# PSUM banks of a mixture-of-experts scatter: from a pool of three to a pool of five

## The chip, the core and the metric

The kernel runs on one core of one Trainium2 chip. Its time is the device time of one launch in microseconds (us). Three runs of the kernel before gave 1573.3, 1576.45 and 1577.18 us; their median is 1576.45 us. TensorE is written PE, VectorE DVE, ScalarE ACT, GpSimd POOL, SyncE SP.

## The reference, cut to what matters

Two layers, each with a mixer, a mixture of experts (MoE) and a gated embedding, over 512 tokens of width 1024. The MoE, which takes most of the time, is this:

```python
expert = g_top * EXPERTS_PER_GROUP + top_i          # 2 of 32 experts for each token
weight = pg_top * top_p
...
def expert_block(args):
    idx, e = args
    xb = x_pad[idx]                                  # gather
    hb = jax.nn.silu(xb @ w_gate[e]) * (xb @ w_up[e])
    return hb @ w_down[e]
...
contrib = y_blocks.reshape(-1, d) * w_pad[:, None].astype(x.dtype)
y = jnp.zeros((n + 1, d), x.dtype).at[tok_pad].add(contrib)   # scatter
```

`w_gate` and `w_up` are 1024x512 and `w_down` is 512x1024, all fp32, so the weights of one expert are 6.29 MB and those of a layer's 32 experts 201 MB. All of them are read in each layer.

## The kernel before, in words

The MoE walks over the 32 experts in 16 pairs (`Moe.run`, L993). Each expert has 64 slots for tokens, so that a pair fills 128 partitions. For a pair, PE does in this order:

- `gate_up` (L949) of both experts: the fp32 products with the gate and up weights (L961), one PSUM bank for each expert. ACT (L965) and DVE (L967) make `hh` of it.
- the scatter of the pair before it, in eight chunks of 128 tokens by 512 columns (`scatter`, L853). A chunk takes a bank; PE adds two products into it, with the 0/1 matrix `sg` as weights (L857 with the high part `yh`, L858 with the low part `yl`), and DVE adds the bank to the residual `h` (L860). The chunks are spread: two (`some(2)`, L1027), later three (`some(3)`, L1042), later the remaining three (`some(8)`, L1047).
- between them: `slots` (L940, four tiny products, read by DVE at L942); two halves of the gather for the next four experts (L919 and L920, sixteen products for a bank, copied out by ACT or DVE in `evac`, L923: the first half of a pair by ACT, the second by DVE); and two transposes each of `hh` (`turn`, L974, copied out by ACT at L976).
- `down` (L979): the products with the down weights (L987) into two banks, which ACT (L867) and DVE (L868) weigh into `yh` and `yl`.

Pairs 0 to 13 hold gathers, 14 and 15 don't. Pair 0 has nothing to scatter. In pair 13 the scatter runs in one piece ahead of a test for overflowing experts (`overflow`, L1070), which waits for a value that the engines load into registers. In pairs 9 to 12 a slice of the embedding product (`emb`, L1177) stands between the second gather half and the last three chunks; pair 8 has transposes of the embedding's input (L1160) between `slots` and the gather.

PSUM has eight banks. One pool, named psum, hands them out under two tags: `acc` has five of them and `aux` three. Each tag hands its banks out in turn, and a tile that takes a bank waits until the readers of the tile that had it are done:

```python
def acc(shape, dt=F32):
    return psum.tile(shape, dt, name="acc", tag="acc", bufs=5)

def aux(shape, dt=F32):
    return psum.tile(shape, dt, name="aux", tag="aux", bufs=3)
```

`acc` serves `gate_up` and `down` (four tiles in a pair); `aux` serves everything else. So a pair with gathers takes `aux` in this order: chunk, chunk, slots, gather half, transposes, transposes, chunk, chunk, chunk, gather half, chunk, chunk, chunk.

The weights come through a ring of SBUF slots of 1 MB (`Loader`, L44). SP issues the loads in the order of use, each as soon as its slot is free; a slot is free when the products that read it are done. A gate-and-up slot is loaded by two DMAs of 512 KB, a down slot by one of 1 MB. From pair 4 on (`late`, L889) there are fewer slots. Everything is written in the order in which the engines run it (`manual_schedule`).

Of the kernel before, what the change touches and what calls it, by code (L numbers as in the profile page):

```python
# [21 lines left out]
P = 128  # L22
S = 512
T = S // P
# [195 lines left out]
def hybrid_encoder(ctx, tc, A, out):  # L220
# [20 lines left out]
    def aux(shape, dt=F32):  # L241
        return psum.tile(shape, dt, name="aux", tag="aux", bufs=3)
# [607 lines left out]
        v.tensor_scalar_min(ovt[:, 0:1], ovt[:, 0:1], float(NE - 1))  # L850
        v.tensor_copy(ove, ovt[:, 0:1])

    def scatter(sg, yh, yl, tiles=range(T), parts=range(2)):  # L853
        for t in tiles:
            for n in parts:
                ps = aux([P, 512])
                nc.tensor.matmul(ps, sg[:, t * P:(t + 1) * P], yh[:, n * 512:(n + 1) * 512], start=True, stop=False)  # L857
                nc.tensor.matmul(ps, sg[:, t * P:(t + 1) * P], yl[:, n * 512:(n + 1) * 512], start=False, stop=True)  # L858
                hv = h[:, t, n * 512:(n + 1) * 512]
                nc.vector.tensor_tensor(hv, ps, hv, op=ALU.add)  # L860

    def weigh(spot, yps, ws):
        y = spot[0].tile([P, 2, D], F32R, name="y_" + spot[1], tag=spot[1])
        yh, yl = y[:, 0], y[:, 1]
        for n in range(2):
            sl = slice(n * 512, (n + 1) * 512)
            nc.scalar.activation(yh[:, sl], yps[n], AF.Copy, scale=ws)  # L867
            nc.vector.scalar_tensor_tensor(yl[:, sl], yps[n], ws, yh[:, sl], op0=ALU.mult, op1=ALU.subtract)  # L868
        return yh, yl

    class Moe:
# [121 lines left out]
        def run(self, router, tail):  # L993
            self.Rs[0] = R0
            self.new_xt(0)
            for kp in range(4):
                self.evac(self.xts[0], kp, router.banks[kp])
            pend = None
            for pr in range(NE // 2):
                b = pr // 2  # L1000
                last = pr == NE // 2 - 1
                more = b + 1 < NE // 4
                if pr == 4:
                    self.late()
                if pr and pr % 2 == 0 and more:
                    self.batch_prep(b + 1)
                if pr:
                    hA = self.gate_up(2 * pr)
                    hB = self.gate_up(2 * pr + 1)
                else:  # L1010
                    hA, spot = self.claim(self.gate_up, 0)
                    self.marks(spot)
                    self.batch_prep(1)
                    hB, spot = self.claim(self.gate_up, 1)
                    self.spots.append(spot)
                todo = [(t, n) for t in range(T) for n in range(2)] if pend else []
                if pr == 13:
                    scatter(*pend)
                    todo = []
                    overflow(self.i, self.ex, self.wo, self.yspot, self.sgs)  # L1020

                def some(k):
                    for t, n in todo[:k]:
                        scatter(*pend, [t], [n])
                    del todo[:k]

                some(2)  # L1027
                ws, sg = self.slots(pr)
                if pr == 5:
                    self.ple.loads(self.wo)  # L1030
                if pr == 8:
                    self.ple.turn_p()
                    self.ple.fetch(0)
                if more:
                    if pr % 2 == 0:
                        self.new_xt(b + 1)
                    self.gather(b + 1, [2 * (pr % 2)])
                else:
                    some(1)
                tA = self.turn(hA)  # L1040
                tB = self.turn(hB)
                some(3)  # L1042
                if more:
                    self.gather(b + 1, [2 * (pr % 2) + 1])
                if 9 <= pr < 13:
                    self.ple.emb(pr - 9)
                some(8)  # L1047
                if last:
                    self.rs.close()
                    self.egs.close()  # L1050
                    tail()
                if pr:
                    yps = self.down([tA, tB])
                else:
                    yps, self.yspot = self.claim(self.down, [tA, tB])
                yh, yl = weigh(self.yspot, yps, ws)
                pend = (sg, yh, yl)
                if 8 <= pr < 12:
                    self.ple.part()
                    if pr < 11:  # L1060
                        self.ple.fetch(pr - 7)
            self.pend = pend

        def finish(self, t):
            scatter(*self.pend, [t])
            if t == T - 1:
                L.open([self.yspot, self.mspot])
                self.exs.close()
# [203 lines left out]
    for i in range(2):  # L1272
# [47 lines left out]
        def tail():  # L1320
            ple.head(moe.spots[1])
# [84 lines left out]
```

## Time and profile before

| | us |
|---|---|
| median of three runs | 1576.45 |
| lowest and highest | 1573.3 and 1577.18 |
| profiled execution | 1572.59 |
| its span | 1570.6 |
| PE busy in the span | 1487.9 (95%) |
| DVE, ACT, POOL busy | 691.4, 375.2, 183.2 |
| bytes moved | 457.35 MB, 291 GB/s on the mean |
| MoE of layer 0, pairs 1 to 15 | 249.3 to 715.5 |

A busy PE is not PE at its peak, since the recorded products overlap: a row of PE that starts 0.23 us after the one before it can be 0.40 us long. Therefore the distance between starts says what a product costs, and a distance that is longer than elsewhere says that PE waited. In the timeline, `x4` merges four instructions into one row, from the start of the first to the end of the last. PEld is PE's weight load, which runs ahead of the product and shows the wait for a bank first. `PEclk` is the clock that PE was granted, 1.00 being 2.4 GHz. The DMA share is the busy share of the 16 DMA engines, which can come out a little over 1.

### The profile page before, as it was taken

What the parts mean: (1) busy time and instruction counts of PE and PEld (TensorE: products, weight loads), DVE (VectorE), ACT (ScalarE), POOL (GpSimd) and SP (SyncE); (2) the same over time, 40 slices, a digit from 0 to 9 for tenths busy, and PEclk for the clock granted to TensorE, in tenths of its full rate; (3) what the DMA queues carried; (4) which work ended last, traced back from release to release, by engine and by line L of the source; (5) the groups of instructions that cost most, each with busy time, mean ns of one, the idle gap of its engine ahead of it and who ended that gap; (6) DMA issues with size and microseconds to landing.
All of it is one profiled execution on the core that took longest, in us unless ns stands there. A gap on an engine that the chain in (4) does not pass through costs nothing. (4 is left out here: it accounts for less than half of the span.)

```text
span 1570.6 us, 19212 instructions
## 1 busy us (share of the span) xinstructions
PE 1487.9 (95%) x7510; PEld 896.9 (57%) x7510; DVE 691.4 (44%) x1165; ACT 375.2 (24%) x686; POOL 183.2 (12%) x271
## 2 busy tenths in 40 slices
PE   6999989999999999999898899899999999998997
PEld 5888865445444554436686678554454445544366
DVE  4554362323333332236779974623233333232266
ACT  4222231101011111015356653211011011110043
POOL 3300040000000000001346531400000000000011
PEclk9999999999999999999999999999999999999999
DMA  9432559989999999997122246599899999998951
GB/s 308 127 99 89 214 184 349 393 330 412 412 411 404 386 385 379 379 415 260 55 81 81 81 134 232 204 346 395 327 412 412 413 399 391 388 367 332 410 197 54
DMA packets 130100, 457.35 MB, mean 291 GB/s; under 512 B 11845, under 2 KB 36629, under 8 KB 113621
## 3 DMA queue, kind: packets, MB, share of 16 engines
q1 hardware_dynamic: 128036, 450.22, 74.9%
q0 software_dynamic: 1824, 5.58, 1.1%
q8 instruction: 62, 1.02, 0.3%
q14 instruction: 34, 0.27, 0.0%
q10 hardware_dynamic: 144, 0.26, 0.0%
HBM read 453.91 MB, written 2.10 MB: 290 GB/s over the span
## 5 line engine op out<-in xcount | busy, mean ns | idle before, releaser
L987 PE MATMUL acc<-slot_base,ht 128*64 128x512 f32 x728 | 205.9, 595 | 0.0
L967 DVE TENSOR_TENSOR hh<-acc,sl 128x256 f32<-128x256 f32 x64 | 39.7, 620 | 369.0 <-ACT sl L965 369.0
L860 DVE TENSOR_TENSOR h<-aux,h 128x512 f32<-128x512 f32 x256 | 161.2, 681 | 72.8 <-PE aux L858 72.8
L868 DVE SCALAR_TENSOR_TENSOR y_base<-acc,ws,y_base 128x512 fp32r<-128x512 f32 x64 | 48.1, 751 | 195.1 <-ACT y_base L867 192.3
L961 PE MATMUL acc<-slot_base,xt_xt 128*64 128x512 f32 x592 | 132.3, 592 | 0.0
L961 PE MATMUL acc<-slot_base,xt_base 128*64 128x512 f32 x528 | 119.9, 593 | 1.2 <-DMA slot_base<-in_w_exp_up_dram 1.2
L965 ACT ACTIVATE sl<-acc 128x256 f32<-128x256 f32 x64 | 24.5, 383 | 397.5 <-PE acc L961 397.5
L857 PE MATMUL aux<-y_base,marks 128*128 128x512 f32 x256 | 111.3, 435 | 8.1 <-ACT xt_base L927 2.9
L867 ACT ACTIVATE y_base<-acc,ws 128x512 fp32r<-128x512 f32 x64 | 44.0, 687 | 304.1 <-issue 227.2
L987 PEld LDWEIGHTS acc<-slot_base,ht 128*64 128x64 f32 x728 | 62.9, 137 | 88.4 <-issue 81.2
L858 PE MATMUL aux<-y_base,marks 128*128 128x512 f32 x256 | 101.6, 397 | 0.8 <-DVE y_base L868 0.6
L961 PEld LDWEIGHTS acc<-slot_base,xt_xt 128*64 128x64 f32 x592 | 42.4, 137 | 84.1 <-issue 81.1
L961 PEld LDWEIGHTS acc<-slot_base,xt_base 128*64 128x64 f32 x528 | 37.9, 137 | 77.3 <-issue 75.0
L857 PEld LDWEIGHTS aux<-y_base,marks 128*128 128x128 f32 x256 | 48.0, 187 | 58.3 <-issue 24.3
L485 PE MATMUL acc<-x_x,pair_base 128*128 128x512 f32 (+1 forms) x208 | 78.6, 378 | 1.0 <-DVE x_x L473 1.0
L484 PE MATMUL acc<-x_x,pair_base 128*128 128x512 f32 (+1 forms) x208 | 78.8, 379 | 0.0
L486 PE MATMUL acc<-x_x,pair_base 128*128 128x512 f32 (+1 forms) x208 | 78.4, 377 | 0.0
L919 PE MATMUL aux<-marks,x_z 128*128 128x256 f32 x256 | 67.1, 299 | 3.4 <-DVE h L860 2.4
L445 POOL TENSOR_SCALAR ss<-ss 128x1 f32<-128x1 f32 x28 | 8.8, 314 | 512.6 <-ACT junk L443 512.5
L486 PE MATMUL acc<-pair_base,x_z 128*128 128x512 f32 (+1 forms) x164 | 64.0, 390 | 1.0 <-DVE x_z L481 1.0
L484 PE MATMUL acc<-pair_base,x_z 128*128 128x512 f32 (+1 forms) x164 | 64.5, 394 | 0.1
L920 PE MATMUL aux<-marks,x_z 128*128 128x256 f32 x256 | 63.9, 286 | 0.1
(289 smaller groups left out, 2833.5 us busy)
## 6 DMA issues: line engine op xcount, KB each, us to landing
slot_base<-in_w_exp_down_dram SPq DMA_DIRECT2D x91, 1024.0 KB, 12.2
slot_base<-in_w_exp_gate_dram SPq DMA_DIRECT2D x140, 512.0 KB, 10.2
slot_base<-in_w_exp_up_dram SPq DMA_DIRECT2D x140, 512.0 KB, 10.2
slot_late<-in_w_exp_down_dram SPq DMA_DIRECT2D x20, 1024.0 KB, 12.6
slot_late<-in_w_exp_gate_dram SPq DMA_DIRECT2D x36, 512.0 KB, 10.3
slot_late<-in_w_exp_up_dram SPq DMA_DIRECT2D x36, 512.0 KB, 10.4
slot_early<-in_w_exp_gate_dram SPq DMA_DIRECT2D x29, 512.0 KB, 10.2
slot_early<-in_w_exp_up_dram SPq DMA_DIRECT2D x29, 512.0 KB, 10.2
```

Source lines behind the costliest of these rows:

```text
L484: nc.tensor.matmul(ps, lh, rh, start=first, stop=False)
L485: nc.tensor.matmul(ps, lh, rl, start=False, stop=False)
L486: nc.tensor.matmul(ps, ll, rh, start=False, stop=last)
L857: nc.tensor.matmul(ps, sg[:, t * P:(t + 1) * P], yh[:, n * 512:(n + 1) * 512], start=True, stop=False)
L858: nc.tensor.matmul(ps, sg[:, t * P:(t + 1) * P], yl[:, n * 512:(n + 1) * 512], start=False, stop=True)
L860: nc.vector.tensor_tensor(hv, ps, hv, op=ALU.add)
L867: nc.scalar.activation(yh[:, sl], yps[n], AF.Copy, scale=ws)
L868: nc.vector.scalar_tensor_tensor(yl[:, sl], yps[n], ws, yh[:, sl], op0=ALU.mult, op1=ALU.subtract)
L919: nc.tensor.matmul(ps[:, kk], X.h(t, k), rv, start=(t == 0), stop=False)
L920: nc.tensor.matmul(ps[:, kk], X.l(t, k), rv, start=False, stop=(t == T - 1))
L961: nc.tensor.matmul(ps[hf * C:(hf + 1) * C].rearrange("p (g f) -> p g f", g=2), xt[:, k, lo:lo + C], rv[:, :, kk, hf * 256:(hf + 1) * 256], ...
L987: nc.tensor.matmul(yps[n][a * C:(a + 1) * C], hts[a][:, j, half], rv[:, j, n * 512:(n + 1) * 512], start=(half == 0 and j == 0), stop=(hal ...
```

## The change

The scatter's chunks in `Moe.run`'s spread (`some`) take `acc` tiles instead of `aux` tiles. The scatters in pair 13, in the overflow loop and in `finish` keep `aux`. The numbers of banks stay five and three.

```diff
-    def scatter(sg, yh, yl, tiles=range(T), parts=range(2)):
+    def scatter(sg, yh, yl, tiles=range(T), parts=range(2), wide=False):
         for t in tiles:
             for n in parts:
-                ps = aux([P, 512])
+                ps = (acc if wide else aux)([P, 512])
...
                 def some(k):
                     for t, n in todo[:k]:
-                        scatter(*pend, [t], [n])
+                        scatter(*pend, [t], [n], True)
                     del todo[:k]
```

No instruction moves. What changes is which semaphores PE's instructions wait for. On PE in pair 1, from the first two chunks (L857, L858) over `slots` (L940) to the first product of the gather (L919), before:

```order
L857 MATMUL aux<-y_base_1960,marks 128x512 [waits DVE_49,Activation_49]
L858 MATMUL aux<-y_base_1960,marks 128x512 [waits DVE_49]
L857 MATMUL aux<-y_base_1960,marks 128x512 [waits Activation_49]
L858 MATMUL aux<-y_base_1960,marks 128x512 [waits DVE_49]
L940 MATMUL aux<-wx,R_142 128x6 [waits PE_49]
L940 MATMUL aux<-wx,R_142 128x6 x3
L919 MATMUL aux<-marks,x_z_394 128x256 [waits DVE_49]
```

and in the changed kernel:

```order
L857 MATMUL acc<-y_base_1960,marks 128x512 [waits DVE_49,Activation_49]
L858 MATMUL acc<-y_base_1960,marks 128x512 [waits DVE_49]
L857 MATMUL acc<-y_base_1960,marks 128x512 [waits Activation_49]
L858 MATMUL acc<-y_base_1960,marks 128x512 [waits DVE_49]
L940 MATMUL aux<-wx,R_142 128x6 x4
L919 MATMUL aux<-marks,x_z_394 128x256
```

The gather no longer waits for DVE, whose L860 had to empty the bank of the first chunk.

On PE in the same pair, from the transposes (L974) over the next three chunks to the second gather half, before:

```order
L974 MATMUL aux<-ident,hh 128x128
L857 MATMUL aux<-y_base_1960,marks 128x512 [waits Activation_49]
L858 MATMUL aux<-y_base_1960,marks 128x512
L857 MATMUL aux<-y_base_1960,marks 128x512 [waits Activation_49]
L858 MATMUL aux<-y_base_1960,marks 128x512
L857 MATMUL aux<-y_base_1960,marks 128x512 [waits Activation_49]
L858 MATMUL aux<-y_base_1960,marks 128x512
L919 MATMUL aux<-marks,x_z_394 128x256 [waits DVE_49]
```

and in the changed kernel:

```order
L974 MATMUL aux<-ident,hh 128x128
L857 MATMUL acc<-y_base_1960,marks 128x512 [waits PE_49]
L858 MATMUL acc<-y_base_1960,marks 128x512
L857 MATMUL acc<-y_base_1960,marks 128x512 [waits Activation_49]
L858 MATMUL acc<-y_base_1960,marks 128x512
L857 MATMUL acc<-y_base_1960,marks 128x512 [waits Activation_49]
L858 MATMUL acc<-y_base_1960,marks 128x512
L919 MATMUL aux<-marks,x_z_394 128x256 [waits Activation_49]
```

The first of these chunks waited for ACT's copy of the first gather half; now it waits for PE's own products of the pair before. The gather half waited for the DVE add of the first of the three chunks; now for ACT's copy of the first gather half.

On PE at the end of that scatter, from the last chunk to the first down products (L987), before:

```order
L857 MATMUL aux<-y_base_1960,marks 128x512 [waits DVE_49]
L858 MATMUL aux<-y_base_1960,marks 128x512
L987 MATMUL acc<-slot_spare_1862,ht 64x512 [waits DMAHW1_49]
L987 MATMUL acc<-slot_base_1868,ht 64x512 [waits DMAHW2_49]
L987 MATMUL acc<-slot_spare_1862,ht 64x512
```

and in the changed kernel:

```order
L857 MATMUL acc<-y_base_1960,marks 128x512 [waits DVE_49]
L858 MATMUL acc<-y_base_1960,marks 128x512
L987 MATMUL acc<-slot_spare_1862,ht 64x512 [waits DMAHW1_49,DVE_49,Activation_49]
L987 MATMUL acc<-slot_base_1868,ht 64x512 [waits DMAHW2_49,Activation_49]
L987 MATMUL acc<-slot_spare_1862,ht 64x512 [waits DVE_49]
```

The down products, which waited for their weights alone, now also wait for DVE and ACT. The first product of `gate_up` gets such a wait for DVE too.

## Rows read from the trace of the kernel before

**Rows 1.** The page, busy us of PE, share of the span, instructions.
```profile
PE 1487.9 (95%) x7510; PEld 896.9 (57%) x7510; DVE 691.4 (44%) x1165; ACT 375.2 (24%) x686; POOL 183.2 (12%) x271
```

**Rows 2.** Waits of PEld: line, waited for, us in total, times, longest.
```profile
PEld aux L919 <- DVE h L860: 14.2, 46, 0.3
...
PEld aux L857 <- ACT xt_base L927: 5.7, 12, 0.5
PEld aux L857 <- ACT xt_xt L927: 5.7, 12, 0.5
```

**Rows 3.** Timeline, PE, scatter of pair 6: start, us, instruction, idle before.
```profile
416.94 0.50 PE L940 MATMUL aux<-wx,marks 128*128 128x6 f32 x4
417.69 0.39 PE L919 MATMUL aux<-R,x_z 128*128 128x256 f32 x1 [0.24 <-DVE h L860]
...
419.71 0.60 PE L974 MATMUL aux<-ident,hh 128*128 128x128 f32 x4
420.55 0.50 PE L857 MATMUL aux<-y_base,marks 128*128 128x512 f32 x1 [0.24 <-ACT xt_xt L927]
420.88 0.39 PE L858 MATMUL aux<-y_base,marks 128*128 128x512 f32 x1
421.11 0.39 PE L857 MATMUL aux<-y_base,marks 128*128 128x512 f32 x1
...
422.06 0.39 PE L919 MATMUL aux<-R,x_z 128*128 128x256 f32 x1
422.28 0.28 PE L920 MATMUL aux<-R,x_z 128*128 128x256 f32 x1
422.40 0.28 PE L919 MATMUL aux<-R,x_z 128*128 128x256 f32 x1
...
425.02 0.50 PE L857 MATMUL aux<-y_base,marks 128*128 128x512 f32 x1
425.36 0.40 PE L858 MATMUL aux<-y_base,marks 128*128 128x512 f32 x1
```

**Rows 4.** Timeline, PE, pair 0, from slots to the gather.
```profile
237.06 0.61 PE L940 MATMUL aux<-wx,R 128*128 128x6 f32 x4
237.53 0.36 PE L919 MATMUL aux<-marks,x_z 128*128 128x256 f32 x1
```

**Rows 5.** Timeline, PE, pair 8, from the embedding's transposes to the gather.
```profile
478.77 1.25 PE L1160 MATMUL aux<-ident,praw 128*128 128x128 f32 x8 [0.25 <-DVE h L860]
479.78 0.37 PE L919 MATMUL aux<-marks,x_z 128*128 128x256 f32 x1
```

**Rows 6.** Stretches, layer 0, pairs 1-4, 5-8, 9-12, 13-15: last three PEclk, DMA share, GB/s.
```profile
249.30:371.40 122.10, 120.15 (x610) 57.53 (x608) 39.04 (x76) 13.03 (x29) 2.35 (x3) 1.00 0.96 373
371.40:494.60 123.20, 121.25 (x618) 58.40 (x616) 40.27 (x78) 14.32 (x31) 0.00 (x0) 1.00 1.02 411
494.60:627.80 133.20, 131.25 (x706) 69.09 (x704) 41.83 (x80) 19.87 (x41) 2.14 (x3) 1.00 0.99 386
627.80:715.50 87.70, 83.72 (x394) 34.80 (x390) 25.92 (x49) 8.57 (x20) 0.00 (x0) 1.00 0.95 371
```

**Rows 7.** Timeline, SP, issue of the last gate-and-up load of pair 7.
```profile
431.91 0.33 SPq L72 DMA_DIRECT2D slot_late<-in_w_exp_up_dram  x1
```

**Rows 8.** Timeline, PE, products of that load: the second eight of sixteen.
```profile
442.90 3.60 PE L961 MATMUL acc<-slot_late,xt_base 128*64 128x512 f32 x16
```

**Rows 9.** Timeline, SP, issue of the last gate-and-up load of pair 15.
```profile
690.83 0.33 SPq L72 DMA_DIRECT2D slot_spare<-in_w_exp_up_dram  x1
```

**Rows 10.** Timeline, PE, products of that load, eight.
```profile
701.08 1.94 PE L961 MATMUL acc<-slot_spare,xt_base 128*64 128x512 f32 x8 [0.51 <-DMA slot_spare<-in_w_exp_up_dram]
```

**Rows 11.** Timeline, DVE, adds of the middle three chunks of pair 6.
```profile
421.31 1.89 DVE L860 TENSOR_TENSOR h<-aux,h 128x512 f32<-128x512 f32 x3 [2.14 <-PE aux L858]
```

**Rows 12.** Line L857: semaphore instructions of its own, ns each.
```profile
L857 PEldq EVENT_SEMAPHORE  x30: 51/51/51, 258.8 to 1501.3; - x30
```

**Rows 13.** Stretch around the overflow test of layer 1, columns as in rows 6.
```profile
1430.00:1440.30 10.30, 4.54 (x23) 4.34 (x22) 2.34 (x7) 0.00 (x0) 0.00 (x0) 0.67 1.03 407
```

## Prediction, made before the changed kernel ran

> **What bounds the kernel now.** I read the page first: PE is busy for 1487.9 of 1570.6 us, 95%, so little can be won that is not won on PE [rows 1]. Then the waits of PE's weight loads, filtered for the scatter's and the gather's lines. The reader is to see many short waits at two places for other engines to empty a bank: 46 times 0.3 us at the gather's first product for the DVE add of a chunk, and twice 12 times 0.5 us at a chunk for ACT's copy of a gather half [rows 2]. Then the timeline of one pair, where the distances between starts show what each wait costs [rows 3], and two places of the same program where the same step has no such wait [rows 4, 5]. Last the stretches of the MoE, because PE is not alone: in pairs 5 to 8 the DMA engines are busy all the time (share 1.02, 411 GB/s), in the other pairs nearly (0.95 to 0.99, but 371 to 386 GB/s) [rows 6]. PE sets the pace, and the weights run just ahead of it. Layer 1 is built and timed alike, so I count layer 0 and double it.
>
> **What the change removes, on PE.** In a pair with gathers three banks rotate over thirteen tiles; each wait below comes from that.
>
> First gather half. L919 starts at 417.69, 0.25 us after the end of the four `slots` products (416.94 + 0.50) [rows 3]. In pair 0, which has no chunk, it starts at 237.53, 0.14 before their end (237.06 + 0.61) [rows 4]. The wait costs 0.39. Afterwards its bank is that of a transpose of the pair before: long free.
>
> Middle chunks. L857 starts at 420.55, 0.24 after the end of the transposes (419.71 + 0.60), released by ACT [rows 3]. Where a product follows transposes without a wait, it starts 0.24 before their end (479.78 against 478.77 + 1.25) [rows 5]. That is 0.48. Afterwards the bank is one of the pair before's down products, which had to be emptied into `yh` and `yl` before any chunk could begin.
>
> Second gather half. It starts in step, but its second product follows 0.22 after the first, where the next follow at 0.12 (422.06, 422.28, 422.40) [rows 3]: 0.10, the weight load that could not run ahead. Afterwards it waits for ACT's copy of the first half, which ended before 420.55.
>
> Last chunk. L858 follows L857 by 0.34 (425.02, 425.36), where 0.23 is the step (420.88, 421.11) [rows 3]: 0.11, in pairs 1 to 8. In pairs 9 to 12 the embedding stands between and there is nothing to gain there.
>
> Sum: 1.08, with the same small refill at the first two places 1.1 us in each of pairs 1 to 8, 1.0 in pairs 9 to 12. Pairs 14 and 15 have the like waits without a gather; I put them at 1.0. Pair 13 and pair 0 stay. On PE alone that is 8 x 1.1 + 4 x 1.0 + 2 x 1.0 = 14.8 us a layer, 29.6 in all.
>
> **What it adds.** Five banks now serve twelve tiles of a pair in turn: each takes the bank of the fifth before it. Followed round, the two down tiles take those of the second and third middle chunk, `gate_up` of the next pair those of the first two of the last three, the middle chunks those of a down tile and of `gate_up`. The tightest is the first down product, behind which all of `down` and then the next `gate_up` are queued. The DVE adds of the middle chunks end at 421.31 + 1.89 = 423.20 [rows 11], and the last chunk's second product, ahead of `down`, starts at 425.36 [rows 3]: over 2 us to spare, of which the change eats 1.1. In pairs 14 and 15, where five chunks follow each other, little is to spare; a wait there would be a part of one add, 0.63 (1.89 / 3), and it would stand beside a wait for weights. A third semaphore in one instruction costs a semaphore instruction of 51 ns [rows 12], one at `down` and one at `gate_up`: from nothing to 0.1 us a pair, 28 x 0.1 = 3 us. I take nothing, since PE's queue runs ahead of its products there; the 3 us stay in the range.
>
> **What of it lasts.** A pair's weights are 12.58 MB (two experts, three matrices of 1024 x 512 fp32). At 411 GB/s, the highest of the four stretches, they take 30.6 us. Against that, pair by pair [rows 6]:
>
> Pairs 1 to 4 take 30.5 us each (122.1 / 4) and live partly on a stock: 373 x 122.1 gives 45.5 MB, 50.3 are used. The rate leaves room. The whole 4 x 1.1 = 4.4 counts.
>
> Pairs 5 to 8 take 30.8, the transfers 30.6. Nothing is left but the reserve. The last load of pair 7 is issued at 431.91 [rows 7] and used from 442.90 + 1.7 (half of 3.60 less the tail) = 444.6 [rows 8], 12.7 later. In pair 15, where PE does wait for it, the like load is issued at 690.83 [rows 9] and used at 701.08 [rows 10], 10.25 later. The reserve is 2.4 us, and of 4.4 us only that counts.
>
> Pairs 9 to 12 take 33.3 (133.2 / 4). The embedding's slice adds 0.26 MB; 12.84 MB at 411 GB/s are 31.2. PE would need 32.3. All 4.0 count.
>
> Pairs 13 to 15: PE already waits for weights at the end [rows 10]. Nothing counts, and the gains of pairs 14 and 15 are lost.
>
> 4.4 + 2.4 + 4.0 = 10.8 a layer, 21.6 us in all. The profiled execution took 1572.6 (span 1570.6); it would take 1551.0. The median of the runs lies 3.9 higher, at 1576.45: 1554.9, and I say 1555.
>
> The Trainium skill speaks against the step on pairs 5 to 8 and 9 to 12 in both directions. Its page DMA: Bandwidth & Descriptors, section "Where 436 GB/s comes from", says that loads from HBM are bound at about 358 GB/s for a core, and names 435 GB/s as the ceiling on the SBUF side. The rows contradict the first: 411 GB/s over 123 us; by it a pair would take 35.1 us already and nothing could be won. By the second a pair's weights take 28.9 us (an estimate from that page), and pairs 5 to 8 would keep all; that is the first rival's time.
>
> **Rivals.**
> All of it lasts. 411 GB/s is then not a limit of the transfers but what PE's releases of slots allow; PE's pace and the transfers' agree within 0.2 us in pairs 5 to 8, which looks like one following the other. Against it: share 1.02, no lower stretch between. 29.6 us: 1546.9, near 1547.
>
> The gap behind the transposes is their own and not the bank's. For it: it is 0.24 each time. Against it: ACT is named as the releaser, and behind the transposes of pair 8 there is none [rows 3, 5]. Then 0.6 a pair is left, 12 x 0.6 = 7.2 a layer, within the reserve: 14.4, near 1562.
>
> The transfers set the time throughout, as shares of 0.95 to 1.02 could say, and PE waits at weights instead of banks. Then nothing changes: 1574 to 1577. Against it: three stretches move 371 to 386 GB/s beside one of 411.
>
> Slower. With the reserve gone PE stops for weights in the middle of `gate_up`, and its clock falls to 1.2 GHz behind each stop. At the overflow test of layer 1 PE was busy for 4.54 of 10.3 us and was granted 0.67 of its clock: about 3.4 us lost [rows 13]. One such fall in pairs 6, 7, 8, 14 and 15 of both layers is 10 x 3.4 = 34 us against 21.6 won, so 1576.45 + 12.4 = 1589. It decides once a stop comes near those 5.8 us; I expect at most 1 us, and the 0.5 us stop of pair 15 left PEclk at 1.00 [rows 6, 10]. The page TensorE: Matmul & The Clock Gate, section "HAM oscillation — how this bites in real kernels", tells of waits for transfers between bursts of products that bring the clock down.
>
> That the change does nothing to the banks is ruled out: the semaphores that PE waits for are others.
>
> **How the numbers follow.** My forecast 0.55 (own range 1550 to 1560, for the 3 us of semaphores and the runs' spread); all lasts 0.15; only 0.6 a pair 0.17; no change 0.08; slower 0.05. Under 0.3% (4.7 us) a measurement of this kernel can't tell from no change. Faster: 0.55 + 0.15 + 0.17 = 0.87; same 0.08; slower 0.05. The range 1545 to 1567 leaves out the last two cases.
>
> **What would show it.** Right: no waits of L919 for L860 and of L857 for L927; between transposes and L857 no gap; pairs 1 to 4 at 29.4 us each; new waits of L961 for DMA, under 1 us, in pairs 6 to 9; pairs 5 to 8 still near 30.3 each at 411 GB/s; pairs 9 to 12 at 32.3. Wrong: pairs 5 to 8 faster than 30 us with more than 411 GB/s (first rival); a gap of 0.24 still behind the transposes (second); waits of L987 or L961 for DVE; a granted clock below 1.00 in pairs 6 to 15.

## Result and the profile after

The changed kernel takes 1551.19 us (median of 4 runs, 1550.03 to 1552.96); the kernel before took 1573.3 to 1577.18 in the runs beside it, and one run of 6049.92 us is left out as disturbed. The ratio is 0.9855, 95% interval 0.9835 to 0.9876: about 23 us faster (25 by the two medians, from three and four runs). Run again in a second session it took 1552.06, ratio 0.9860 (0.9840 to 0.9881). Forecast were 1555, and 1545 to 1567. The profiled execution took 1552.06, span 1550.1, against 1572.6 and 1570.6: 20.5 us less, where the sum had 21.6.

The page, busy time of the engines as in [rows 1]:

```profile
PE 1473.7 (95%) x7510; PEld 900.1 (58%) x7510; DVE 691.2 (45%) x1165; ACT 375.0 (24%) x686; POOL 182.9 (12%) x271
```

PE's busy time falls by 14.2 us although it does the same 7510 products: part of a wait is listed as work. The first product of the second gather half lasts 0.39 us in [rows 3] and 0.28 below.

The timeline of PE in pair 6, the places of [rows 3]:

```profile
411.12 0.50 PE L940 MATMUL aux<-wx,marks 128*128 128x6 f32 x4
411.48 0.37 PE L919 MATMUL aux<-R,x_z 128*128 128x256 f32 x1
...
413.48 0.60 PE L974 MATMUL aux<-ident,hh 128*128 128x128 f32 x4
413.84 0.48 PE L857 MATMUL acc<-y_base,marks 128*128 128x512 f32 x1
...
415.31 0.28 PE L919 MATMUL aux<-R,x_z 128*128 128x256 f32 x1
415.43 0.28 PE L920 MATMUL aux<-R,x_z 128*128 128x256 f32 x1
...
418.14 0.39 PE L857 MATMUL acc<-y_base,marks 128*128 128x512 f32 x1
418.36 0.39 PE L858 MATMUL acc<-y_base,marks 128*128 128x512 f32 x1
418.68 0.64 PE L987 MATMUL acc<-slot_late,ht 128*64 128x512 f32 x1
```

Read start against start, here and in [rows 3]. From the slots products to the gather 0.36 instead of 0.75; from the transposes to the middle chunk 0.36 instead of 0.84; at the second gather half 0.12 instead of 0.22; in the last chunk 0.22 instead of 0.34. That is 0.39, 0.48, 0.10 and 0.12, together 1.09 us; steps that are 0.01 or 0.02 shorter at other places make it about 1.2. The first product of `down` follows 0.32 behind the last chunk's second product, as before: the bank that it takes is free.

The waits of the weight loads, as in [rows 2] (line, waited for, us in total, times, longest); the rows of L919 for L860 and of L857 for L927 are gone, and of L860 there are left:

```profile
PEld acc L987 <- DVE h L860: 6.3, 20, 0.4
...
PEld aux L857 <- DVE h L860: 3.8, 10, 0.8
```

The second is pair 13, which keeps the three banks. The first is new, and here a wait view misleads: 20 waits of 0.3 us are put down to a chunk's add in front of `down`, but the distance from chunk to `down` is 0.32 or 0.33 in every pair with spread chunks, before and after. The weight load was as idle there before, with another name beside it. Pair 6 before, then after:

```profile
425.68 0.13 PEld L987 LDWEIGHTS acc<-slot_late,ht 128*64 128x64 f32 x1 [0.37 <-DMA slot_early<-in_w_exp_gate_dram]
```

```profile
418.68 0.13 PEld L987 LDWEIGHTS acc<-slot_late,ht 128*64 128x64 f32 x1 [0.35 <-issue]
```

The same four stretches as [rows 6], pairs 1 to 4, 5 to 8, 9 to 12, 13 to 15 of layer 0 (last three columns: granted clock, DMA share, GB/s):

```profile
249.30:366.70 117.40, 117.40 (x610) 57.78 (x608) 39.04 (x76) 13.06 (x29) 2.35 (x3) 1.00 0.97 383
366.70:487.70 121.00, 119.46 (x618) 58.53 (x616) 40.24 (x78) 14.21 (x31) 0.00 (x0) 1.00 1.02 412
487.70:617.30 129.60, 129.15 (x706) 69.16 (x704) 41.83 (x80) 19.90 (x41) 2.14 (x3) 1.00 1.02 405
617.30:704.40 87.10, 82.05 (x394) 35.18 (x390) 25.73 (x49) 8.61 (x20) 0.00 (x0) 1.00 0.96 375
```

Against [rows 6] they are 4.7, 2.2, 3.6 and 0.6 us shorter. In the first PE is busy without a hole. In the second the transfers move 412 GB/s, as before, and PE has 1.5 us of holes. What it waits for in the MoE of layer 0, 249 to 700 us (us in total, times, longest):

```profile
PE acc L961 <- DMA slot_base<-in_w_exp_up_dram: 2.1, 4, 0.6
...
PE acc L961 <- DMA slot_spare<-in_w_exp_up_dram: 1.0, 2, 0.5
PE acc L961 <- DMA slot_late<-in_w_exp_up_dram: 0.5, 1, 0.5
```

PE waits for weights seven times, for at most 0.6 us each; before there were two such waits in this layer.

Last the long stretches: in the kernel before, pairs 1 to 15 of layer 0, the dense part between the two MoEs, pairs 1 to 15 of layer 1:

```profile
249.30:715.50 466.20, 456.38 (x2322) 219.82 (x2318) 147.05 (x283) 55.79 (x118) 4.48 (x6) 1.00 0.98 386
715.50:1033.00 317.50, 288.52 (x1450) 228.31 (x1448) 232.16 (x319) 156.03 (x257) 116.65 (x120) 0.98 0.43 146
1033.00:1505.10 472.10, 458.04 (x2320) 221.63 (x2318) 147.01 (x283) 55.76 (x118) 4.47 (x6) 0.99 0.97 381
```

and after:

```profile
249.30:704.40 455.10, 448.06 (x2322) 220.65 (x2318) 146.84 (x283) 55.78 (x118) 4.48 (x6) 1.00 1.00 396
704.40:1024.30 319.90, 289.74 (x1450) 228.89 (x1448) 232.31 (x319) 155.87 (x257) 116.46 (x120) 0.97 0.42 145
1024.30:1484.60 460.30, 450.19 (x2322) 222.75 (x2318) 146.82 (x283) 55.80 (x118) 4.47 (x6) 0.99 0.98 391
```

The MoEs win 11.1 and 11.8 us. The dense part, which the change does not touch, takes 2.4 more at a mean clock of 0.97 instead of 0.98: together 20.5.

### The profile page after: what moved, and what is told of

Read it like the earlier page. It is cut to its first block, busy times and chain, and to the rows that moved or that the text cites. A ratio compares the mean times of both kernels' runs of the same rounds, so it can differ in the third digit from the quotient of the medians.

```text
span 1550.1 us, 19252 instructions
## 1 busy us (share of the span) xinstructions
PE 1473.7 (95%) x7510; PEld 900.1 (58%) x7510; DVE 691.2 (45%) x1165; ACT 375.0 (24%) x686; POOL 182.9 (12%) x271
## 3 DMA queue, kind: packets, MB, share of 16 engines
q8 instruction: 62, 1.02, 0.3%
## 5 line engine op out<-in xcount | busy, mean ns | idle before, releaser
L987 PE MATMUL acc<-slot_base,ht 128*64 128x512 f32 x728 | 205.9, 595 | 0.0
L860 DVE TENSOR_TENSOR h<-acc,h 128x512 f32<-128x512 f32 x224 | 140.7, 681 | 50.4 <-PE acc L858 50.4
L987 PEld LDWEIGHTS acc<-slot_base,ht 128*64 128x64 f32 x728 | 62.9, 137 | 87.9 <-issue 80.5
L857 PE MATMUL acc<-y_base,marks 128*128 128x512 f32 x224 | 93.8, 419 | 0.0
L858 PE MATMUL acc<-y_base,marks 128*128 128x512 f32 x224 | 88.2, 394 | 0.0
L919 PE MATMUL aux<-marks,x_z 128*128 128x256 f32 x256 | 65.3, 292 | 2.5 <-issue 1.8
L484 PE MATMUL acc<-pair_base,x_z 128*128 128x512 f32 (+1 forms) x164 | 64.5, 393 | 0.2
L486 PE MATMUL acc<-pair_base,x_z 128*128 128x512 f32 (+1 forms) x164 | 63.6, 388 | 0.8 <-DVE x_z L481 0.8
L485 PE MATMUL acc<-pair_base,x_z 128*128 128x512 f32 (+1 forms) x164 | 63.6, 388 | 0.0
## 6 DMA issues: line engine op xcount, KB each, us to landing
slot_late<-in_w_exp_up_dram SPq DMA_DIRECT2D x36, 512.0 KB, 10.8
```

Source lines behind the costliest of these rows:

```text
L484: nc.tensor.matmul(ps, lh, rh, start=first, stop=False)
L485: nc.tensor.matmul(ps, lh, rl, start=False, stop=False)
L486: nc.tensor.matmul(ps, ll, rh, start=False, stop=last)
L919: nc.tensor.matmul(ps[:, kk], X.h(t, k), rv, start=(t == 0), stop=False)
L987: nc.tensor.matmul(yps[n][a * C:(a + 1) * C], hts[a][:, j, half], rv[:, j, n * 512:(n + 1) * 512], start=(half == 0 and j == 0), stop=(hal ...
```

## Experiments

Theory: each bank wait that goes is PE time won, and the transfers, at 412 GB/s, keep back what PE could have won in pairs 5 to 8 and near the end. All ratios are to the kernel before on the same chip: median 1573.99 of 11 runs for the two halves of the change and for the kernel that moves the slots and the gather, 1574.81 of 17 runs for the others. The parts of the change come first.

### Only the first two chunks

`some(k)` gets an argument that picks the banks; the second half of the experiment is the next one.

```
-                some(2)
+                some(2, True)      # five banks; the other calls of some() keep three
```

> Only the first two chunks of a pair take the five banks; the six behind the gather's first half stay with the three. Theory (each place has its own wait, and each wait removed is PE time won until the transfers bind): the wait of the first gather half for a chunk's add, 0.39 us behind the slots products, goes, and all else stays (0.39 behind the transposes, 0.10 at the second gather half, 0.10 at the last chunk). 0.40 x 14 pairs = 5.6 us a layer; pairs 5 to 8 win 1.6, less than the reserve of 2.2 to 2.4, so that lasts; pairs 14 and 15 (0.7) do not. 4.9 a layer, about 10 us in all: 1566 to 1567. Rival (a wait that is removed comes back at the next place: the middle chunk waits for a bank anyway): the gap behind the transposes grows from 0.39 to near 0.8 and the time stays at 1575 to 1577.

Measured: 1564.81 us (1560.3 to 1568.45, 6 runs), ratio 0.9932 (0.9914 to 0.9949): 10.7 us by the ratio, where about 10 was expected. PE's timeline in pair 6:

```profile
415.92 0.50 PE L940 MATMUL aux<-wx,marks 128*128 128x6 f32 x4
416.28 0.36 PE L919 MATMUL aux<-R,x_z 128*128 128x256 f32 x1
...
418.29 0.60 PE L974 MATMUL aux<-ident,hh 128*128 128x128 f32 x4
419.13 0.50 PE L857 MATMUL aux<-y_base,marks 128*128 128x512 f32 x1 [0.24 <-ACT xt_xt L927]
```

The wait in front of the gather is gone (0.36), the one behind the transposes is what it was (0.84), no longer. A wait that is taken away does not come back at the next place: the rival is out. Pairs 5 to 8:

```profile
370.80:492.40 121.60, 120.64 (x618) 58.12 (x616) 40.23 (x78) 14.22 (x31) 0.00 (x0) 1.00 1.02 412
```

They win 1.6 us, all of 4 x 0.40.

### Only the later six chunks

```
-                some(2)
+                some(2, False)     # three banks; the other calls of some() take five
```

> The other half of the change: the first two chunks stay with the three banks, the later six take the five. Theory: the 0.39 behind the slots products stays; the 0.39 behind the transposes (down to nothing), the 0.10 at the second gather half and the 0.10 at the last chunk go: 0.61 x 8 + 0.51 x 4 + 0.6 x 2 = 8.1 us of PE a layer, of which pairs 5 to 8 keep 2.2 to 2.4 of 2.4 and pairs 14 and 15 nothing: 6.9 a layer, 14 us in all: 1562 to 1563. With the first two alone (10 us) that makes 24, more than the 20 to 25 of the whole change only by what pairs 5 to 8 can't keep of both: on the trace, pairs 5 to 8 gain 1.6 and 2.3 a layer one by one, and 2.2 together. Rival (no limit of the transfers: what is missing from the whole change's 32 us is lost elsewhere): pairs 5 to 8 gain 1.6 and 2.4 one by one and 4.0 or more together is what PE should give, and the parts fall short of their own PE sum by the same share as the whole. Rival (gaps behind the transposes belong to the transposes): 0.2 a pair, 1571.

Measured: 1560.3 us (1557.23 to 1564.7, 6 runs), ratio 0.9908 (0.9888 to 0.9927): 14.5 us by the ratio, where 14 was expected. The mirror image in pair 6, 0.76 in front of the gather and 0.36 behind the transposes:

```profile
413.45 0.50 PE L940 MATMUL aux<-wx,marks 128*128 128x6 f32 x4
414.21 0.39 PE L919 MATMUL aux<-R,x_z 128*128 128x256 f32 x1 [0.26 <-DVE h L860]
...
416.23 0.60 PE L974 MATMUL aux<-ident,hh 128*128 128x128 f32 x4
416.59 0.48 PE L857 MATMUL acc<-y_base,marks 128*128 128x512 f32 x1
```

From the last product of `gate_up` to the first of `down` a pair takes 0.40 us less in the first experiment, 0.77 here, 1.18 in the whole change (10.31, 9.92, 9.54, 9.13): on PE the parts add up. I had expected 0.61 here; the gap behind the transposes is 0.48, as in the prediction, and I had used 0.39. The parts do not add up in the pairs that are bound by transfers; pairs 5 to 8:

```profile
368.70:489.60 120.90, 119.36 (x618) 58.80 (x616) 40.23 (x78) 14.30 (x31) 0.00 (x0) 1.00 1.02 412
```

PE's own gain is 3.1 (4 x 0.77), 2.3 of it last, and the whole change with 4.7 on PE does not come lower than 121.0 (120.8 in the second session). Over pairs 1 to 15 of both layers the parts win 11.6 and 16.4 us, 28.0 in sum, the whole change 22.9. Of the 5.1 between them 3.2 lie in pairs 5 to 8 and 0.7 in pairs 9 to 12. Another 1.8 lie in pair 13, which differs from kernel to kernel for a reason that stays open (last section); pairs 14 and 15 make up for 0.5. By the times alone (10.7 and 14.5 by the ratios, against 22.0) the sum could not be told from the whole, given their intervals of some 3 us each.

### Only the three middle chunks

```
-                        scatter(*pend, [t], [n], True)
+                        scatter(*pend, [t], [n], (t, n) in ((1, 0), (1, 1), (2, 0)))
```

> Only the three middle chunks take the five banks. Theory: the wait behind the transposes (0.48) and the refill at the second gather half (0.10) go, the wait of the first gather half (0.39) and the 0.10 at the last chunk stay: 0.58 to 0.66 us a pair on the trace, of which pairs 5 to 8 keep all but a few tenths. One look, so the time says only 1560 to 1568. Rival (the gap is the transposes' own, or the chunk then waits for the pair before's yh/yl): 0.1 to 0.3 a pair.

A single run: 1556.57 us, below the 1560 to 1568 that was expected. PE's timeline of pair 6:

```profile
418.02 0.60 PE L974 MATMUL aux<-ident,hh 128*128 128x128 f32 x4
418.37 0.48 PE L857 MATMUL acc<-y_base,marks 128*128 128x512 f32 x1
```

The gap behind the transposes is gone (0.35). A pair takes 9.69 us instead of 10.31, 0.62 less, in the range of the theory: the 0.48 and the 0.10 at the second gather half, which move together here. The 0.15 by which the six chunks win more (0.77) is that of the last chunk. Pairs 5 to 8:

```profile
370.30:491.20 120.90, 119.88 (x618) 58.46 (x616) 40.23 (x78) 14.33 (x31) 0.00 (x0) 1.00 1.02 412
```

Three kernels, whose PE could have won 2.5, 3.1 and 4.7 us here, end at 120.9, 120.9 and 121.0, all at 412 GB/s. That looks like a floor, though this kernel, with 2.5, says little of it (in layer 1 it keeps all of it), and the next one, with 3.4, ends at 120.6. Whether the floor is the transfers' the lighter ones below tell. By time this version looks faster than that with six chunks, without being so on PE: in the profiled executions its dense part between the MoEs took 317.5 us, the other's 320.4.

### The slots and the gather move instead

The chunks stay with three banks; L940 and the gather's tile in front of L919 take the five.

```
-                ps = aux([P, 2, 4 * C])
+                ps = acc([P, 2, 4 * C])
...
-            ps = aux([P, 6])
+            ps = acc([P, 6])
```

> The scatter chunks stay with the three banks; the slots product and both gather halves take the five instead (7 tiles a pair over five banks, 10 over three). Theory (the cost is thirteen tiles in three banks, whichever they are): the waits behind the slots products and behind the first chunk's tile go as in the change; at most the second middle chunk waits for ACT's copy of a transpose, up to 0.3 us a pair (28 x 0.3 = 8). So between the change's time and 8 above: 1551 to 1559. Rival (it has to be the chunks that leave, since their adds on DVE are what is waited for): the gather's half no longer waits, but the chunks still wait for each other's adds and for the transposes' copies at each place: 0.6 or more of the 1.2 a pair stays: 1562 or above.

Measured: 1556.91 us (1554.78 to 1565.27, 6 runs), ratio 0.9891 (0.9869 to 0.9914). The weight loads' waits name the one wait that costs time now, 31 times (before 4 times, in pairs 14 and 15):

```profile
PEld aux L857 <- ACT ht L976: 13.0, 31, 0.5
```

PE's timeline of pair 6 shows what it costs:

```profile
414.81 0.60 PE L974 MATMUL aux<-ident,hh 128*128 128x128 f32 x4
415.16 0.48 PE L857 MATMUL aux<-y_base,marks 128*128 128x512 f32 x1
415.48 0.40 PE L858 MATMUL aux<-y_base,marks 128*128 128x512 f32 x1
415.92 0.50 PE L857 MATMUL aux<-y_base,marks 128*128 128x512 f32 x1
```

The first middle chunk follows the transposes at 0.35; the second starts 0.44 behind the first's second product where 0.23 is the step, because it takes the bank of a transpose that ACT is still copying. A pair takes 9.46 us: 0.85 of the 1.18 is won without moving a chunk. So the cost came from thirteen tiles in three banks, and it is not the chunks as such. Nor is it their number alone: the kernel with the three middle chunks moved leaves ten tiles in three banks too, and it wins 0.62. In that kernel the wait that stays in front of the gather is for a DVE add, here it is a chunk's wait for ACT's copy of a transpose: it also counts which tile had the bank that comes next. The rival, that 0.6 or more would stay, is out for the pairs with a gather (0.33 stays). In pairs 14 and 15, which have no gather, a pair takes 6.26 to 6.31 us where the change takes 5.3 and before 6.52 to 6.58: there it does have to be the chunks.

### Lighter transfers, before and after

In both kernels each down load brings half of its rows; the other half of the down weights is left out of the sums, and the number of products stays.

```
-  L.loads.append(("dn", [(lambda t: t.rearrange("p (j d) -> p j d", d=D), src)]))
+  L.loads.append(("dn", [(lambda t: t[:, :D].rearrange("p (j d) -> p j d", d=D), src[:, :1])]))
...
-                                             rv[:, j, n * 512:(n + 1) * 512],
+                                             rv[:, 0, n * 512:(n + 1) * 512],
```

> The kernel before with only half of each down matrix loaded (0.52 MB in place of 1.05 MB per load, the same number of loads, slots and products; both halves of a sum use the half that is there): 10.5 MB a pair, 25.5 us at 411 GB/s, so transfers bind nowhere in the MoE. PE's work and its waits for banks stay: every theory expects no more than the few waits for weights of before to go, 1572 to 1577; the pairs 1 to 8 near 30.5 us each.

> The changed kernel with the same half of each down matrix left out. Theory (the transfers take what the whole change does not keep): now every pair keeps its 1.2 us: 8 x 1.18 + 4 x 1.08 + 2 x 1.2 = 16.2 a layer, less about 1 at pair 13: 30 to 32 us below the light kernel before, with pairs 5 to 8 gaining 4.7 instead of 2.3 and no waits of L961 for DMA. Rival (the missing 10 us are lost elsewhere, the transfers only look busy): 20 to 23 us below it, pairs 5 to 8 gaining 2.3 as in the full kernel.

Measured: light before 1572.59 us (1570.65 to 1577.04, 12 runs), ratio 0.9988 (0.9977 to 0.9998); light after 1542.15 (1540.52 to 1545.81, 5 runs), ratio 0.9801 (0.9785 to 0.9818). The change is now worth 30.4 us by the medians and 29.4 by the ratios; the theory said 30 to 32. Over pairs 1 to 15 of both layers the two profiles differ by 31.2 us. Pairs 1 to 4, 5 to 8 and 9 to 12 of layer 0, light before:

```profile
252.10:374.20 122.10, 120.16 (x610) 57.53 (x608) 39.05 (x76) 13.03 (x29) 2.35 (x3) 1.00 0.88 330
374.20:497.40 123.20, 121.27 (x618) 58.37 (x616) 40.24 (x78) 14.35 (x31) 0.00 (x0) 1.00 0.88 328
497.40:630.60 133.20, 131.25 (x706) 69.05 (x704) 41.81 (x80) 19.88 (x41) 2.14 (x3) 1.00 0.85 321
```

and light after:

```profile
249.30:366.70 117.40, 117.40 (x610) 57.78 (x608) 39.02 (x76) 13.05 (x29) 2.35 (x3) 1.00 0.91 339
366.70:485.20 118.50, 118.50 (x618) 58.63 (x616) 40.23 (x78) 14.22 (x31) 0.00 (x0) 1.00 0.92 345
485.20:614.10 128.90, 128.90 (x706) 69.26 (x704) 41.80 (x80) 19.89 (x41) 2.14 (x3) 1.00 0.87 332
```

Light before is, stretch for stretch, as long as before [rows 6]: in these three the transfers cost nothing yet. Light after wins 4.7, 4.7 and 4.3 instead of 4.7, 2.2 and 3.6, PE has no hole in any of the three, and no wait for weights is left. So the missing time of pairs 5 to 12 was the transfers'. The rival, that it is lost elsewhere, is out.

### Also the chunks of pair 13 and of the last pair

```
-                    scatter(*pend)
+                    scatter(*pend, wide=True)
...
-            scatter(*self.pend, [t])
+            scatter(*self.pend, [t], wide=True)
```

> The change, and also the two places that it left with three banks: the eight chunks in a row in pair 13 and those of the last pair in the phase behind the MoE. In pair 13 PE waits 0.57 us once and 0.10 at each chunk, about 1.2 us, but behind them the overflow test holds PE, and in this stretch the transfers bind. If the test's wait (1.37 us in layer 0) takes that up: no difference from the change, 1550 to 1554. If not: 1 us a layer, 1548 to 1552, too little to tell by time; then the trace of pair 13 shows it.

Measured: 1551.54 us (1550.92 to 1555.0, 4 runs), ratio 0.9860 (0.9843 to 0.9877): the change's time. The slots products of pair 13, behind the overflow test, in the change (in brackets: idle before, released by):

```profile
637.67 0.58 PE L940 MATMUL aux<-wx,R 128*128 128x6 f32 x4 [1.21 <-DVEq L1072]
```

and here:

```profile
637.64 0.58 PE L940 MATMUL aux<-wx,R 128*128 128x6 f32 x4 [2.40 <-DVEq L1072]
```

PE is through with the eight chunks 1.2 us earlier and waits 1.2 us longer for the test, which stands behind DVE's eight adds (4.87 us in both). In layer 0 a wait is only moved. In layer 1 it is not: the wait for the test is no longer than in the change (5.9 us against 6.1), and pair 13 takes 38.0 us instead of 38.9. Whether that is the banks' is not shown, since this pair takes 37.4 to 39.2 us in the kernels of this document. Pair 15 takes 0.3 us longer there and 0.9 in layer 0, so that the MoEs differ by 0.2 us in all. No version here beats the change by its time.

## Why the prediction was right

**The steps on PE.** In front of the first gather half 0.39 was foreseen and 0.39 measured, at the middle chunks 0.48 and 0.48, at the second gather half 0.10 and 0.10, at the last chunk 0.11 and 0.12. They came from start-to-start distances, compared with a place in the same program where the same step has no wait; the idle times shown (0.24 at each of the first two places, none at the others) would have given less than half. The first was shown by itself, the second and third together; the fourth is what the six chunks win beyond the middle three. The rival that gave the gap behind the transposes to the transposes (1562) is out. In pairs 14 and 15 PE won 1.2 and 1.3 us between `gate_up` and `down`, where 1.0 was put.

**What it adds.** Nothing, as taken: with the light transfers a pair of 1 to 7 takes 29.3 to 29.4 us, what the sum gives (30.5 less 1.1), and `gate_up` follows 0.42 behind `down` in both kernels, so neither pays for its new bank neighbours or for a third semaphore. The waits of L987 for DVE, which were to be a sign of being wrong, did appear in the wait view; by the distances they cost nothing.

**What lasts.** Pairs 1 to 4: 4.4 foreseen, 4.7 measured. Pairs 5 to 8: 2.4 foreseen, 2.2 and in layer 1 2.3 measured, so the reserve read from two issue times [rows 7 to 10] had the right size; the kernels with more on PE than that kept 2.2 to 2.7. The rival "all of it lasts" (1547) failed on this step, and the light pair shows that with fewer bytes it would have been right. Of the two limits that the Trainium skill's page DMA: Bandwidth & Descriptors, section "Where 436 GB/s comes from", names, 358 GB/s is exceeded here (412 over 121 us, on the one core that runs) and 435 is not reached: by it the transfers of pairs 5 to 8 would take 115.7 us (an estimate from that page, 4 x 12.58 MB), where 121.0 stand. Pairs 9 to 12: 4.0 foreseen, 3.6 measured: PE starts them without a reserve and waits for weights once more, which the sum, taking the stretch by itself, left out. Pairs 13 to 15: 0 foreseen, 0.6 and 1.4 measured. That PE waits for weights at the end of a stretch [rows 10] does not make all of the stretch theirs: it moves 375 GB/s, not 412. Pair 14 kept its 1.2 us in both layers, pair 15, where the wait for weights is, 0.5 and 0.6 (0.1 in the second session); pair 13 lost 1.1 in layer 0 (last section) and 0.4 in layer 1. Together 10.8 a layer foreseen, 11.1 and 11.8 measured.

**What nothing in the sum had.** The dense part between the MoEs took 2.4 us more. Its length goes with its clock rather than with the banks: 317.5 us at 0.98 before and in the kernel with three chunks moved, 318.5 at 0.97 for the changed kernel run again, 324.0 at 0.96 in the kernel with two, and 322.2 at 0.96 in the lighter kernel before, which moves no tile. The changed kernel run again, and the kernel with two chunks:

```profile
704.40:1022.90 318.50, 290.47 (x1450) 229.38 (x1448) 232.25 (x319) 156.24 (x257) 116.43 (x120) 0.97 0.43 145
```

and

```profile
711.50:1035.50 324.00, 293.51 (x1448) 231.47 (x1448) 234.37 (x319) 155.91 (x257) 117.11 (x120) 0.96 0.42 143
```

That the clock causes all of it is not shown: the same kernel gives 319.9 and 318.5, and the kernel with six chunks 320.4 at 0.98. So it is partly luck that 20.5 us in the profile lie so near the sum's 21.6: the MoEs won 22.9.

**The median.** 1555 came from 1551.0 for the profiled execution, plus the 3.9 by which the profiled one of before lay under its median. That offset was mostly the scatter of three runs: over 11 and 17 runs on two chips the median of before is 1573.99 and 1574.81, and the profiled run of the changed kernel lies 0.9 above its own median. Without it the forecast would have been 1551 to 1553.

**Slower** (1589) did not come near. The new stops for weights are of at most 0.6 us, and in this profile the granted clock stays at 1.00 in all four stretches of layer 0. It need not: in the second session it fell behind the overflow test of pair 13 (0.98 over pairs 13 to 15), which is one of the signs of being wrong. But it fell behind no stop for weights, and pair 13 took no longer than in the first session (last section).

## What to carry to other kernels

Where tiles of several engines rotate in a few banks, read what each wait costs from the distance of two starts against the same step elsewhere, and count how many tiles pass through a group of banks, and look which tile had the bank that comes next: moving some of them to a group with slack took away waits here without a faster engine. Then ask, stretch by stretch, what the next limit allows: work out the reserve of the transfers from issue and use, and credit no more than that. If you want to know who took the rest, make the suspect lighter in both kernels and take the difference again.

## What the runs showed that was not expected

In pair 13 of layer 0, behind the overflow test, the changed kernel lost 1.1 us against before in both profiles, each time in another form. In the first PE sat idle for 1.82 us before a gather product, with nothing named:

```profile
642.51 0.28 PE L919 MATMUL aux<-marks,x_z 128*128 128x256 f32 x1 [1.82 <-issue]
```

In the other it had no such stop and ran the first gather half at the lower clock: the products start 0.21 us apart instead of 0.12, and the granted clock is 0.79 from 638 to 646 us. PE had been idle for 1.21 us just before, as in the first:

```profile
638.60 0.41 PE L920 MATMUL aux<-marks,x_z 128*128 128x256 f32 x1
638.81 0.41 PE L919 MATMUL aux<-marks,x_z 128*128 128x256 f32 x1
```

The lighter kernel after had the stop again (1.78), and so had the kernel that moves the slots and the gather (1.74); those with six and three chunks had a short one (0.6 and 0.4), that with the first two none in this layer, but one of 2.66 us in layer 1. What PE waits for there stays open; it wasn't tried.

The lighter loads moved fewer bytes for the busy time of the DMA engines: light after has 345 GB/s at a DMA share of 0.92 in pairs 5 to 8, which is 375 for a share of 1, the full kernel 412 at 1.02, which is 404. Whether the size of the loads does it is not shown, since the lighter kernel leaves its engines idle part of the time; before, with full loads and a share of 0.96, has 389 in pairs 1 to 4.
